# First stage of a hybrid transformer block as one pass over the blocks of k, with packed weight slabs and weights loaded further ahead

## The chip, the cores and the metric

The kernel runs on one core of a Trainium2 chip. The metric is the device time of one execution in microseconds (us), as the median of several runs. The profile is one further execution; "the span" is the time from its first to its last instruction. Engines are PE (matmuls; PEld is its weight load), DVE (VectorE), ACT (ScalarE), POOL (GpSimd) and SP (which issues most DMAs). PSUM has eight banks of 128 x 512 fp32; a matmul writes into one of them.

## The reference, cut to what matters

```python
def block(x, p, w):                          # S = 512 tokens, D = 1024, one layer
    h = rms_norm(x, ln1_g)                   # fp32
    z = h @ w_in                             # mq mk mv mo mi mf | aq akc avc aks avs akw avw ag
    m = mlstm(mq, mk, mv, mi, mf)            # 4 heads of 128, chunks of 64
    a = nsa(aq, akc, avc, aks, avs, akw, avw, ag, ...)   # 8 heads of 64 in 2 groups:
                                             # compressed, selected and window keys
    x = x + concat(m, a) @ w_out
    x = x + convffn(rms_norm(x, ln2_g))      # width 2048, 3 taps
    return rms_norm(x + ple_gate(...), final_g)

def compress(t, pe, w1, w2):                 # for akc and avc: blocks of 32 tokens, stride 16
    return gelu((blocks(t) + pe) @ w1) @ w2
```

Every product is made in fp32 accuracy from three products of a high and a low part: high x high, low x high and high x low.

## The kernel before, in words

The change touches the first 97 us of the kernel, up to the first attention scores (`s_3b`). There the work is a list of jobs (`Stream`), each the product of one packet of weights with all 512 tokens. A job's weights are loaded by SP into one of two buffers (tag `raw`), ACT copies the high part out (`...h`), DVE subtracts to get the low part (`...l`), and PE runs the three products. While a job runs, only the next one is prepared (`AHEAD`), so a load is issued when a `raw` buffer has been read by ACT and DVE.

- `tok0` to `tok3`, two blocks of k each: token-major columns (selected and window values `avs`, `avw`, gates), 288 wide, into four banks (`psA`, tiles `ptm`), one per 128 tokens.
- `c0`, `c1` (the inputs `akc`, `avc` of the compression), `k0`, `k1` (keys), `q00`, `q01` (queries): 128 columns each, feature-major into one bank (`pc`, `pk`, `pq`), 24 matmuls of 512 columns.
- `w00` to `w11` (tiles `cw00` to `cw11`): first matrix of the compression of akc (0) and avc (1), each in two halves.
- `m0` to `m3` (tiles `mv0` to `mv3`): the values of the mLSTM, token-major, into four banks.

`ORDER` lists them: c0 k0 c1 k1 q00 w00 q01 w01 m0 w10 m1 w11 m2 m3. Events run between jobs by estimated time (`st.after`), on engines that each work strictly in their written order. The row factors of the norm come from the squares (`sq`, `acc`), a matmul `n1ps`, a Newton iteration on DVE (`n1v` to `n1yc`), and a matmul `n1pb` that spreads them for feature-major results (`n1rb`, copied by ACT). `token_evac` scales the token-major results (`V` by ACT and DVE, `gz` by DVE). `cmp_evac` scales a result `pc` (`zc`), moves it by four DMAs on ACT's queue into `cA` (lines 409 and 410), adds the positions (`cX`, four pieces on DVE) and splits the sum (`cXh` on ACT, `cXl` on DVE). `mlstm_gates` transposes `gz` on PE (`pgt`), and makes running sums on DVE (two scans); `mlstm_gate_columns` transposes the sums on PE (`pgc`) and DVE copies them (`gcol`). `cmp_gelu` (tile `hc`) and `cmp_turn` (a transpose `pct` on PE, copied to `gt`) follow the last half of a compression. `pgt`, `pgc`, `pct` and `pc2` share one PSUM bank, V, which holds one of them at a time:

```python
def cmp_turn(kv, h2):
    pt = pV(f"pct{kv}")
    TE.transpose(pt[:, 0:62], h2, ident[0:62, 0:62])
```

Evacuated keys and queries are copied to their places by DMAs on POOL (line 386).

Of the kernel before, what the change touches and what calls it, by code (L numbers as in the profile page):

```python
# [27 lines left out]
ORDER = "c0 k0 c1 k1 q00 w00 q01 w01 m0 w10 m1 w11 m2 m3"  # L28
T_TE = 4.0
T_GC = 14.0  # L30
T_CT = 6
# [8 lines left out]
GATES = "k0"  # L40
AHEAD = (1, 1)
# [12 lines left out]
C_G1, C_G2, C_G3, C_GF = 0, 8, 16, 24  # L54
C_CW, C_CB = 32, 80
C_MG = 96
C_PK, C_PV = 100, 116
C_VALID = 132
N_COLS = 133
# [7 lines left out]
def hybrid_block_kernel(ctx: ExitStack, tc: tile.TileContext, a, out):  # L67
# [39 lines left out]
    cols = consts.tile([128, N_COLS], F32, name="cols")  # L107
    xbuf = main.tile([128, KB, S], F32, tag="B16", bufs=3, name="xT")
# [8 lines left out]
    def split(name, src_ap, shape):  # L117
        raw = wpool.tile(shape, F32, tag="raw", bufs=2, name=name + "r")
        hi = wpool.tile(shape, F32R, tag="hi", name=name + "h")
        lo = wpool.tile(shape, F32R, tag="lo", name=name + "l")  # L120
        n = 1 if name == "tok0" else shape[1]
        for i in range(0, shape[1], n):
            nc.sync.dma_start(raw[:, i:i + n], src_ap[:, i:i + n])
            SE.activation(hi[:, i:i + n], raw[:, i:i + n], AF.Copy)
            VE.tensor_sub(lo[:, i:i + n], raw[:, i:i + n], f32(hi[:, i:i + n]))
        return hi, lo

# [5 lines left out]
    class Stream:  # L133
        """The matrix products in their order on the tensor engine; events run between them."""

        def __init__(self):
            self.jobs, self.ready, self.cur, self.done = [], [], None, set()
            self.now, self.events, self.debt = 0.0, [], 0.0
# [3 lines left out]

        def prepare(self, depth):
            while len(self.ready) < depth and self.jobs:
                name, src, shape, run = self.jobs.pop(0)
                self.ready.append((name, run, split(name, src, shape)))
# [10 lines left out]
        def step(self):  # L157
            if self.cur is None:
                self.prepare(1)
                if not self.ready:  # L160
                    return None
                name, run, w = self.ready.pop(0)
                self.cur = (name, run(*w))
                self.prepare(AHEAD[self.now > 100])
            try:
                t = next(self.cur[1])
            except StopIteration:
                self.done.add(self.cur[0])
# [69 lines left out]
    def newton_rsqrt(v, w, name):  # L238
        """1 / sqrt(v): a first guess from the bits, a step of third order, which leaves 8/3 of it, and Newton's."""
# [71 lines left out]

    psA = four("ptm")
    for c in range(4):
        st.add(f"tok{c}", a["w_tok"][:, 2 * c:2 * c + 2], [128, 2, 288], tokens_job(psA, 2 * c, 288))
    nc.sync.dma_start(cols, a["cols"])
    nc.sync.dma_start(xbuf[:, 0], a["xT"][:, 0])
    st.prepare(1)
    nc.sync.dma_start(xbuf[:, 1], a["xT"][:, 1])
    for c in range(4):
# [7 lines left out]
        if c == 0:  # L327
            load_consts()
# [21 lines left out]
    def gemm(ps, wh, wl, kw, rh, rl, kx, first=True, last=True, n=slice(0, S)):  # L350
        """kw, kx: the blocks of the weights and of the activations; the low parts of the weights come last."""
# [23 lines left out]
    mixa = main.tile([128, 2, 4, S], F32R, tag="mixa", name="mixa")  # L375
# [101 lines left out]
    # queries: [high; low] for the first pass, [high; position and mask rows] for the second  # L477
# [89 lines left out]
    # mLSTM gates: the running sum of log f, the running maximum, and their columns by token  # L567
# [210 lines left out]
    nc.sync.dma_start(X, a["xT"])  # L778
# [362 lines left out]
def _layouts(inp):  # L1141
# [10 lines left out]
    def percol(v):  # L1152
# [3 lines left out]
    arr["xT"] = c(x.T.reshape(8, 128, S).transpose(1, 0, 2))  # L1156
# [5 lines left out]
    order = ["aks", "akw", "akc", "avc", "aq", "mq", "mk", "mo"]  # L1162
    arr["w_in"] = c(blocks(np.concatenate([cut[n] for n in order], 1)))
    tok = np.concatenate([cut[n] for n in ("avs", "avw", "mi", "mf", "ag")], 1)
    arr["w_tok"] = c(tok.reshape(8, 128, 288).transpose(1, 0, 2))
# [25 lines left out]
    arr["mask"] = np.where(q <= p, 0, NEG).astype(f)
# [30 lines left out]
```

## Time and profile before

| | |
|---|---|
| time, median of 3 runs | 652.88 us (652.25 to 653.68) |
| span of the profiled execution | 651.60 us |
| PE busy | 96% of the span |
| DVE busy | 65% |
| ACT busy | 48% |
| first 80 us: PE busy | 68.68 of 80 us |

The profiled execution's time is known as its span, 651.60 us; it lies 1.28 us under the median of the runs, which contain what lies around the span. Busy shares are means over all stages. What the change moves lies in the first 97 us, so its worth is read from the waits of that stretch and from what PE does there, at which granted clock.

### The profile page before, as it was taken

The page shows a single profiled execution, that of the slowest core. Times are in us where ns is not written, and L with a number is a line of the kernel's source. Part 1 is how long each engine was busy: PE and PEld are TensorE (multiplying, and loading weights), DVE is VectorE, ACT ScalarE, POOL GpSimd, SP SyncE. Part 2 cuts the span into 40 slices and gives each one's busy share as a digit, 9 for nine tenths or more (in the row PEclk, how much of TensorE's full clock was granted, in tenths as well). Part 3 has the DMA queues.
Part 4 walks back from the last instruction along what each step waited for, and adds up shares of the span by engine and source line. Part 5 has one row for each costly group of instructions (what it writes and reads, how often), then busy time and mean ns, then how long its engine had stood idle before and what let it go on. Part 6 is the DMA issues. An engine that isn't in the chain of part 4 may idle for free.

```text
span 651.6 us, 8628 instructions
## 1 busy us (share of the span) xinstructions
PE 626.2 (96%) x3090; PEld 507.3 (78%) x3090; DVE 423.0 (65%) x862; ACT 311.9 (48%) x650; POOL 51.2 (8%) x112
## 2 busy tenths in 40 slices
PE   6899899999999999999999999999999999999993
PEld 6787777777777776787878888888888888888892
DVE  4697538888877977686586555555555434345866
ACT  5544336667657656465545333333333223234542
POOL 1113104211111100000000000000000000000003
PEclk9999799999999999999999999999999999999997
DMA  7676945511112152212233333333333333333203
GB/s 224 183 185 158 209 127 114 114 34 33 55 44 65 34 188 70 66 33 69 82 109 98 97 98 98 97 98 97 98 97 98 97 98 98 97 97 103 92 2 129
DMA packets 22083, 64.85 MB, mean 100 GB/s; under 512 B 2832, under 2 KB 6032, under 8 KB 21844
## 3 DMA queue, kind: packets, MB, share of 16 engines
q1 hardware_dynamic: 18120, 57.55, 30.1%
q0 software_dynamic: 3136, 5.57, 4.9%
q10 hardware_dynamic: 784, 1.18, 0.7%
q8 instruction: 24, 0.39, 0.3%
q14 instruction: 19, 0.16, 0.1%
HBM read 56.42 MB, written 2.10 MB: 90 GB/s over the span
## 4 chain that ended last, share of the span: by engine, by line
PE 80%; DVE 9%; DMA 5%; ACT 3%; issue 2%; SPq 0%; DVEq 0%; POOL 0%; ACTq 0%
PE pu L354 8%; PE pu L355 8%; PE pu L358 8%; PE pd L354 5%; PE pd L355 4%; PE pd L358 4%; PE pt L709 2%; PE pmq L355 2%; PE pmq L358 2%; PE pmq L354 2%; PE pv L717 2%; PE ms L878 2%; PE pmv L299 1%; PE mo L887 1%; PE pg L346 1%
## 5 line engine op out<-in xcount | busy, mean ns | idle before, releaser
L712 ACT ACTIVATE ph<-pt 128x512 fp32r<-128x512 f32 x40 | 23.7, 597 | 20.9 <-PE pt L709 19.5
L1000 ACT ACTIVATE u<-zv 128x512 fp32r<-128x512 f32 x16 | 10.1, 633 | 45.1 <-DVE zv L998 45.1
L713 DVE TENSOR_TENSOR pl<-pt,ph 128x512 fp32r<-128x512 f32 x40 | 27.1, 683 | 6.3 <-ACT ph L712 6.1
L997 DVE TENSOR_TENSOR zv<-pu,n2rb 128x512 f32<-128x512 f32 x16 | 11.1, 691 | 31.0 <-PE pu L358 31.0
L681 POOL TENSOR_SCALAR E<-E,rr 128x512 f32<-128x512 f32 (+3 forms) x32 | 20.3, 634 | 130.5 <-DVE rr L678 87.8
L709 PE MATMUL pt<-ident,E 128*128 128x128 f32 x160 | 27.7, 276 | 0.4 <-DVE E L683 0.3
L987 DVE TENSOR_TENSOR zg<-pu,n2rb 128x512 f32<-128x512 f32 x16 | 11.1, 692 | 26.0 <-PE pu L358 24.6
L1013 DVE TENSOR_TENSOR X<-pd,X 128x512 f32<-128x512 f32 x8 | 5.5, 692 | 31.9 <-PE pd L358 31.9
L709 PEld LDWEIGHTS pt<-ident,E 128*128 128x128 f32 x160 | 19.8, 141 | 7.2 <-DVE E L683 2.1
L990 ACT ACTIVATE cv<-zg,cols 128x512 f32<-128x512 f32 x16 | 13.1, 816 | 20.1 <-DVE zg L987 20.1
L675 ACT ACTIVATE E<-s,nm 128x384 f32<-128x384 f32 (+2 forms) x48 | 22.1, 470 | 0.0
L993 ACT ACTIVATE cv<-cv 128x512 f32<-128x512 f32 x16 | 10.1, 631 | 24.9 <-DVE cv L992 24.9
L986 POOL MEMSET zg<- 128x2 f32 x16 | 1.5, 99 | 245.2 <-DVE cv L992 151.1
L234 DVE TENSOR_TENSOR acc<-acc,sq 128x512 f32<-128x512 f32 (+1 forms) x30 | 19.1, 637 | 1.6 <-ACT sq L230 1.0
L230 ACT ACTIVATE sq<-X 128x512 f32<-128x512 f32 (+1 forms) x24 | 13.5, 561 | 11.0 <-DVE X L1054 11.0
L717 PE MATMUL pv<-ph,V 128*128 128x512 f32 x40 | 18.7, 467 | 0.0
L346 PE MATMUL pg<-x3h,wres 128*128 128x256 f32 x64 | 18.3, 285 | 0.0
L347 PE MATMUL pg<-x3l,wres 128*128 128x256 f32 x64 | 18.1, 283 | 0.0
L348 PE MATMUL pg<-x3h,wres 128*128 128x256 f32 x64 | 18.1, 283 | 0.0
L1001 DVE TENSOR_TENSOR u<-zv,u 128x512 fp32r<-128x512 f32 x16 | 11.1, 692 | 10.5 <-ACT u L1000 10.5
L1094 POOL TENSOR_TENSOR X<-X,n40rb 128x256 f32<-128x256 f32 (+1 forms) x5 | 4.8, 994 | 155.5 <-ACT n40rb L283 155.5
L719 PE MATMUL pv<-pl,V 128*128 128x512 f32 x40 | 16.7, 418 | 0.0
(1077 smaller groups left out, 2044.7 us busy)
## 6 DMA issues: line engine op xcount, KB each, us to landing
Q<-hlq POOLq DMA_DIRECT2D x24, 128.0 KB, 5.8
X<-in_xT SPq DMA_DIRECT2D x1, 2048.0 KB, 7.6
wgr<-in_w_pg SPq DMA_DIRECT2D x4, 512.0 KB, 4.2
xT<-in_xT SPq DMA_DIRECT2D x3, 512.0 KB, 6.5
K<-hlk POOLq DMA_DIRECT2D x12, 128.0 KB, 4.6
out_y<-X SPq DMA_DIRECT2D x5, 256.0 KB, 2.2
out_y<-X SPq DMA_DIRECT2D x5, 128.0 KB, 1.7
Q<-in_qaug POOLq DMA_DIRECT2D x2, 272.0 KB, 6.7
```

Source lines behind the costliest of these rows:

```text
L234: return VE.tensor_add(acc[:, :n], acc[:, :n], sq[:, :n])
L346: TE.matmul(ps, wh[:, kw], rh[:, kx, n], start=first, stop=False)
L347: TE.matmul(ps, wh[:, kw], rl[:, kx, n], start=False, stop=False)
L354: TE.matmul(ps, wh[:, w], rh[:, x, n], start=first and j == 0, stop=False)
L355: TE.matmul(ps, wh[:, w], rl[:, x, n], start=False, stop=False)
L358: TE.matmul(ps, wl[:, w], rh[:, x, n], start=False, stop=last and j == len(kx) - 1)
L675: SE.activation(e, p, AF.Exp, bias=nm[:, b:b + 1], accum_out=rs[:, b:b + 1])
L681: GE.tensor_scalar(e, e, rr[:, b:b + 1], 0.0, op0=ALU.mult, op1=ALU.add)
L709: TE.transpose(pt[:, r * 128:(r + 1) * 128], Es[r][:, c0:c0 + 128], ident)
L712: SE.activation(ph, pt, AF.Copy)
L713: VE.tensor_sub(pl, pt, f32(ph))
L717: TE.matmul(pv, vs, ph, start=first, stop=False)
```

## The change

The host's arrays are repacked. `xg` is the input with the gain of the first norm as a column behind each block of k. `w_s1` has, for each block of k, a slab of 672 columns: the 288 token-major ones, then `akc`, `aks` and `avc`. The small constants go into one array (`cols`, 515 columns), loaded last. Slab 0 is loaded by two DMAs on ACT's queue, all else by SP.

PE starts with nine idle matmuls of 128 x 512 on zeros in bf16 into bank V. Then one pass over the blocks of k in seven banks: for each of the first four blocks (`KO`) 12 token-major matmuls into the four banks `psA` and 9 feature-major ones into `pc0`, `pk0` and `pc1`. The last four blocks follow bank by bank: `first_rest(0)`, the statistics, `first_rest(1)`, `n1pb`, `first_rest(2)`, then the token-major matmuls. `c0`, `c1` and `k0` (and `tok0` to `tok3`) are no jobs any more.

The other loads are issued three jobs ahead (`LOADS`), into four extra 16-KB buffers (`rawx`, in the place of `mixa`, until `mv3` is loaded) besides the two `raw`. The row factors and the evacuations of `pc0` and `pk0` now come in front of the token-major ones. The gates are made by an event 5 us (`T_GATES`) after `token_evac`, and their columns 14 us (`T_GC`, as before) after that.

```diff
-ORDER = "c0 k0 c1 k1 q00 w00 q01 w01 m0 w10 m1 w11 m2 m3"
-T_TE = 4.0
+ORDER = "k1 w00 q00 w01 q01 w10 m0 w11 m1 m2 m3"
+W1 = 288 + 3 * 128
+KO = 4
+NWARM = 9
 T_GC = 14.0
+T_GATES = 5.0
-GATES = "k0"
-AHEAD = (1, 1)
+LOADS = 3
...
+    nc.sync.dma_start(xbuf[:, 0], a["xg"][:, 0])
+    nc.scalar.dma_start(s1raw[0][:, 0, 0:288], a["w_s1"][:, 0, 0:288])
+    nc.scalar.dma_start(s1raw[0][:, 0, 288:W1], a["w_s1"][:, 0, 288:W1])
+    for k, n in ((1, 1), (2, 2), (4, 2), (6, 2)):
+        nc.sync.dma_start(s1raw[k], a["w_s1"][:, k:k + n])
+        nc.sync.dma_start(xbuf[:, k:k + n], a["xg"][:, k:k + n])
+    nc.sync.dma_start(cols, a["cols"])
+    idle = consts.tile([128, 512], BF, name="idle")
+    VE.memset(idle, 0.0)
+    pidle = pV("idle")
+    for _ in range(NWARM):
+        TE.matmul(pidle, idle[:, 0:128], idle, start=True, stop=True)
...
+    def load(name, src_ap, shape):
+        raw = None
+        if early[0]:
+            turn[0] += 1
+            if turn[0] % 6 < 4:
+                raw = early[0][:, turn[0] % 6].rearrange("p (a b) -> p a b", a=shape[1])
+        if raw is None:
+            raw = wpool.tile(shape, F32, tag="raw", bufs=2, name=name + "r")
+        nc.sync.dma_start(raw, src_ap)
+        return raw
...
-                self.prepare(AHEAD[self.now > 100])
+                self.prepare(1)
+                if early[0]:
+                    self.load(LOADS)
...
-    for c in range(4):
-        if c < 3:
-            nc.sync.dma_start(xbuf[:, 2 * c + 2:2 * c + 4], a["xT"][:, 2 * c + 2:2 * c + 4])
-        for k in (2 * c, 2 * c + 1):
-            last = SE.activation(xh[:, k], xbuf[:, k], AF.Copy, scale=cols[:, C_G1 + k:C_G1 + k + 1])
-            VE.scalar_tensor_tensor(xl[:, k], xbuf[:, k], cols[:, C_G1 + k:C_G1 + k + 1], f32(xh[:, k]),
-                                    op0=ALU.mult, op1=ALU.subtract)
-        st.until(f"tok{c}")
+    pairs = ((xh, hi1), (xl, hi1), (xh, lo1))
     for k in range(KB):
-        sq = square(xbuf[:, k], k, acc1)
-        behind(sq, last, "the splits come first")
+        last = first_split(k)
+        if k > 1:
+            square(xbuf[:, k - 2, 0:S], k - 2, acc1)
+        for x, w in pairs if k < KO else ():
+            for t in range(NT):
+                first_tok(k, t, x, w, k == 0 and w is hi1 and x is xh, False)
+            for j in range(3):
+                first_feat(k, j, x, w, k == 0 and w is hi1 and x is xh, False)
...
+    def first_rest(j):
+        for x, w in pairs:
+            for k in range(KO, KB):
+                first_feat(k, j, x, w, False, k == KB - 1 and w is lo1)
+
+    first_rest(0)
     rc1 = rstd_stats(acc1, "n1")
...
-    st.after(T_TE, token_evac)
-    st.until(GATES)
-    mlstm_gates()
-    st.after(T_GC, mlstm_gate_columns)
-    st.until("q01")
-    psM.extend(four("pmv"))
+    early[0] = main.tile([128, 4, 1024], F32, tag="mixa", name="rawx")
+    st.load(2)
+    first_rest(1)
+    rb1 = rstd_rows(rc1, "n1")
+    cmp_evac(0)(psF[0])
+    key_evac(0)(psF[1])
+    first_rest(2)
+    cmp_evac(1)(psF[2])
+    st.prepare(1)
+    st.load(LOADS)
+    for x, w in pairs:
+        for k in range(KO, KB):
+            for t in range(NT):
+                first_tok(k, t, x, w, False, k == KB - 1 and w is lo1)
+    token_evac()
+    st.after(T_GATES, mlstm_gates)
+    st.after(T_GATES + T_GC, mlstm_gate_columns)
     st.until("mv3")
+    mixa = main.tile([128, 2, 4, S], F32R, tag="mixa", name="mixa")
```

The first place is PE around the gate columns. Before, the eight transposes `pgc` of the gates stand inside the products of `q00`, ahead of the first half of the compression of akc:

```order
L358 MATMUL pq_552<-x1h,q00l 128x512 x2
L598 MATMUL pgc<-ident,gi 128x4 x4
L598 MATMUL pgc<-ident,gt 128x4 x4
L358 MATMUL pq_552<-x1h,q00l 128x512 x6
L432 MATMUL pc_606<-cw00h,cXh_384 62x128
```

In the change the same transposes stand in the first half of the compression of avc (`cw10`), shortly ahead of the transpose `pct` of the compression of akc and of the values `mv0` (`ident` is now a part of `cols`):

```order
L490 MATMUL pc_698<-cw10h,cXh_398 62x128
L491 MATMUL pc_698<-cw10h,cXl_400 62x128
L653 MATMUL pgc<-cols,gi 128x4 x4
L653 MATMUL pgc<-cols,gt 128x4 x4
L495 MATMUL pc_698<-cw10l,cXh_398 62x128 x2
L515 MATMUL pct_725<-cols,hc_643 128x62
L495 MATMUL pc_698<-cw10l,cXh_398 62x128 x6
L332 MATMUL pmv_743<-mv0h,x1h 128x512
```

So `pgc` has moved past `q00`, `w00`, `w01` and `q01`, and `pct`, which takes the same bank, now follows it after two matmuls.

The second place is DVE's copy of these columns, `gcol`. Before, it stands after the keys of the second group and before the queries:

```order
L391 TENSOR_TENSOR zk_535<-pk_510,n1rb 128x512
L125 TENSOR_TENSOR cw00l<-cw00r,cw00h 128x1024
L382 TENSOR_TENSOR hlk_537<-zk_535,hlk_537 128x512
L600 COPY gcol<-pgc 128x32
L485 SCALAR_TENSOR_TENSOR zq_589<-pq_552,n1rb 128x512
L125 TENSOR_TENSOR q01l<-q01r,q01h 128x1024
```

In the change it stands behind the queries of both jobs, the splits of `cw10` and `mv0` and the gelu of the compression:

```order
L440 TENSOR_TENSOR hlq_605<-zq_603,hlq_605 128x512
L479 TENSOR_TENSOR cXl_400<-cX_393,cXh_398 128x992
L153 TENSOR_TENSOR cw10l<-rawx,cw10h 128x1024
L505 TENSOR_TENSOR hc_643<-hc_643 62x128
...
L510 TENSOR_TENSOR hc_643<-hc_643 62x128
L543 SCALAR_TENSOR_TENSOR zq_681<-pq_656,n1rb 128x512
L153 TENSOR_TENSOR mv0l<-rawx,mv0h 128x1024
L440 TENSOR_TENSOR hlq_683<-zq_681,hlq_683 128x512
L655 COPY gcol<-pgc 128x32
L517 COPY gt_727<-pct_725 128x62
```

`gcol` is thus the last of this piece, and the copy of `pct` comes right behind it.

The third place is DVE at the row factors. Before, one split (`k0l`) stands between the last addition of squares and the Newton iteration:

```order
L234 TENSOR_TENSOR acc_91<-acc_91,sq 128x512
L125 TENSOR_TENSOR k0l<-k0r,k0h 128x1024
L267 TENSOR_SCALAR n1v<-n1ps 128x4
```

In the change two splits (`k1l`, `cw00l`) stand there, one of them ahead of the last addition:

```order
L265 TENSOR_TENSOR acc_121<-acc_121,sq 128x512
L153 TENSOR_TENSOR k1l<-rawx,k1h 128x1024
L265 TENSOR_TENSOR acc_121<-acc_121,sq 128x512
L153 TENSOR_TENSOR cw00l<-rawx,cw00h 128x1024
L298 TENSOR_SCALAR n1v<-n1ps 128x4
```

The weights of both are now loaded into `rawx` instead of into the two `raw` buffers.

## Rows read from the trace of the kernel before

**Rows 1.** The page's busy time: us, share of the span, instructions.

```profile
PE 626.2 (96%) x3090; PEld 507.3 (78%) x3090; DVE 423.0 (65%) x862; ACT 311.9 (48%) x650; POOL 51.2 (8%) x112
```

**Rows 2.** Waits of PE, first 140 us: total us, times, longest.

```profile
PE pmv L299 <- ACT mv0h L124: 3.1, 1, 3.1
PE n1pb L280 <- issue: 1.9, 1, 1.9
PE pc L354 <- ACT c0h L124: 0.6, 1, 0.6
```

**Rows 3.** Timeline of PE: start us, us, engine, line, out<-in [idle before <-releaser].

```profile
5.63 0.61 PE L299 MATMUL ptm<-tok0h,x1h 128*128 128x288 f32 x1 [5.63 <-ACT tok0h L124]
...
12.04 0.29 PE L300 MATMUL ptm<-tok1h,x1l 128*128 128x288 f32 x1
12.17 0.29 PE L299 MATMUL ptm<-tok1h,x1h 128*128 128x288 f32 x1
...
67.06 0.79 PE L299 MATMUL pmv<-mv0h,x1h 128*128 128x512 f32 x1 [3.07 <-ACT mv0h L124]
...
73.69 1.98 PE L304 MATMUL pmv<-mv0l,x1h 128*128 128x512 f32 x8
...
77.31 0.44 PE L299 MATMUL pmv<-mv1h,x1h 128*128 128x512 f32 x1
...
96.79 0.39 PE L658 MATMUL s_3b<-K,Q 128*128 128x512 f32 x1
```

**Rows 4.** The chain that ended last, at 58 us: start, us, what.

```profile
58.39 7.45 DMA mv0r<-in_w_mv
65.95 1.06 ACT mv0h L124
```

**Rows 5.** Windows: busy us of PE, PEld, DVE, ACT, POOL; granted clock, DMA share, GB/s.

```profile
30.00:40.00 10.00, 9.59 (x49) 7.71 (x49) 7.60 (x18) 4.03 (x8) 0.59 (x2) 1.00 0.52 148
45.00:50.00 5.00, 5.00 (x24) 4.13 (x23) 4.90 (x6) 3.00 (x4) 0.00 (x0) 1.00 0.92 245
50.00:60.00 10.00, 9.95 (x66) 8.12 (x65) 8.90 (x15) 4.58 (x6) 3.92 (x8) 1.00 0.35 88
60.00:70.00 10.00, 6.93 (x43) 5.72 (x42) 4.76 (x5) 2.64 (x3) 4.05 (x9) 0.82 1.29 251
70.00:80.00 10.00, 10.00 (x55) 8.15 (x55) 4.58 (x9) 3.65 (x5) 1.19 (x3) 0.84 0.98 218
```

**Rows 6.** Timeline of SP, its second DMA issue: start us, us.

```profile
1.19 0.42 SPq L316 DMA_DIRECT2D xT<-in_xT  x1
```

**Rows 7.** Lines 409 and 410, the copies into cA, and their landing.

```profile
L409 ACTq DMA_DIRECT2D cA<-zc x4: 469/568/620, 36.0 to 45.7; - x4
DMA to landing us min/median/max: 2.3/2.5/4.2
L410 ACTq DMA_DIRECT2D cA<-zc x4: 610/616/1987, 36.5 to 46.4; - x4
DMA to landing us min/median/max: 2.4/4.5/5.4
```

**Rows 8.** DVE by line and form, first 100 us: busy us, mean ns, idle before.

```profile
L416 DVE TENSOR_TENSOR cX<-cA,cols 128x248 f32<-128x248 f32 x8 | 4.2, 568 | 0.0
L559 DVE SCALAR_TENSOR_TENSOR V<-ptm,n1yc,V 128x256 fp32r<-128x256 f32 x4 | 1.9, 478 | 0.0
L125 DVE TENSOR_TENSOR q01l<-q01r,q01h 128x1024 fp32r<-128x1024 f32 x1 | 1.2, 1203 | 0.0
L584 DVE TENSOR_TENSOR_SCAN gt<-gf,zeroc 4x512 f32<-4x512 f32 x1 | 1.2, 1212 | 0.0
L485 DVE SCALAR_TENSOR_TENSOR zq<-pq,n1rb 128x512 f32<-128x512 f32 x2 | 1.4, 676 | 0.0
L561 DVE TENSOR_SCALAR gz<-ptm,n1yc 128x32 f32<-128x32 f32 x4 | 1.0, 242 | 0.0
L452 DVE TENSOR_TENSOR hc<-hc 62x128 f32<-62x128 f32 x2 | 0.6, 285 | 0.1
```

More of the change, by code (lines that the diff above doesn't have):

```diff
@@ L52 @@
 GELU_A = 0.044715
[L54 to L59, printed above, removed]
+C_G2, C_G3, C_GF = 0, 8, 16
+C_CW, C_CB = 24, 72
+C_MG = 88
+C_PK, C_PV = 92, 108
+C_VALID = 124
+C_SEL, C_GB = 125, 129
+C_ID, C_NEG, C_MASK = 131, 259, 387
+N_COLS = 515
 def f32(ap):
@@ L115, in hybrid_block_kernel, with split @@
     GE.memset(epsc, EPS)
-    def split(name, src_ap, shape):
-        raw = wpool.tile(shape, F32, tag="raw", bufs=2, name=name + "r")
+    turn = [0]
+    def load(name, src_ap, shape):
[8 more added lines that the diff above has]
+        return raw
+    def split(name, raw, shape):
         hi = wpool.tile(shape, F32R, tag="hi", name=name + "h")
         lo = wpool.tile(shape, F32R, tag="lo", name=name + "l")
[L121 to L125, printed above, removed]
+        SE.activation(hi, raw, AF.Copy)
+        VE.tensor_sub(lo, raw, f32(hi))
         return hi, lo
+    early = [None]
     def behind(later, sooner, why, wait=False):
@@ L136, in __init__ @@
         def __init__(self):
-            self.jobs, self.ready, self.cur, self.done = [], [], None, set()
+            self.jobs, self.loaded, self.ready, self.cur, self.done = [], [], [], None, set()
             self.now, self.events, self.debt = 0.0, [], 0.0
@@ L141, in add, with load @@
             self.jobs.append((name, src, shape, run))
+        def load(self, depth):
+            while len(self.loaded) < depth and self.jobs:
+                name, src, shape, run = self.jobs.pop(0)
+                self.loaded.append((name, load(name, src, shape), shape, run))
+                if name == "mv3":
+                    early[0] = None
         def prepare(self, depth):
-            while len(self.ready) < depth and self.jobs:
-                name, src, shape, run = self.jobs.pop(0)
-                self.ready.append((name, run, split(name, src, shape)))
+            while len(self.ready) < depth and (self.jobs or self.loaded):
+                self.load(1)
+                name, raw, shape, run = self.loaded.pop(0)
+                self.ready.append((name, run, split(name, raw, shape)))
         def after(self, us, fn):
@@ L295, in run @@
         def run(wh, wl):
+            if k0 == 0:
+                ps.extend(four("pmv"))
             for k, i in ((k, i) for k in (k0, k0 + 1) for i in range(NT)):
@@ L329, in hybrid_block_kernel, with first_split @@
-    for k in range(KB):
-        sq = square(xbuf[:, k], k, acc1)
-        behind(sq, last, "the splits come first")
+    psF = [pG("pc0"), pG("pk0"), pSb("pc1")]
+    hi1 = main.tile([128, 6, W1], F32R, tag="B16", bufs=3, name="hi1")
+    lo1 = main.tile([128, 6, W1], F32R, tag="B16", bufs=3, name="lo1")
+    def first_split(k):
+        g = xbuf[:, k, S:S + 1]
+        SE.activation(xh[:, k], xbuf[:, k, 0:S], AF.Copy, scale=g)
+        raw = s1raw[min(k, k // 2 * 2) if k > 1 else k]
+        raw = raw[:, k % 2 if k > 1 else 0]
+        for c0, c1 in (((0, 288), (288, W1)) if k == 0 else ((0, W1),)):
+            i = SE.activation(hi1[:, k % 6, c0:c1], raw[:, c0:c1], AF.Copy)
+        VE.scalar_tensor_tensor(xl[:, k], xbuf[:, k, 0:S], g, f32(xh[:, k]), op0=ALU.mult, op1=ALU.subtract)
+        for c0, c1 in (((0, 288), (288, W1)) if k == 0 else ((0, W1),)):
+            VE.tensor_sub(lo1[:, k % 6, c0:c1], raw[:, c0:c1], f32(hi1[:, k % 6, c0:c1]))
+        return i
@@ new lines, in first_tok, with first_feat @@
+    def first_tok(k, t, x, w, start, stop):
+        TE.matmul(psA[t][:, 0:288], x[:, k, t * 128:(t + 1) * 128], w[:, k % 6, 0:288], start=start, stop=stop)
+        st.spend(0.135)
+    def first_feat(k, j, x, w, start, stop):
+        TE.matmul(psF[j], w[:, k % 6, 288 + 128 * j:416 + 128 * j], x[:, k], start=start, stop=stop)
+        st.spend(0.23)
+    pairs = ((xh, hi1), (xl, hi1), (xh, lo1))
+    for k in range(KB):
+        last = first_split(k)
[6 more added lines that the diff above has]
+                first_feat(k, j, x, w, k == 0 and w is hi1 and x is xh, False)
@@ L332, in hybrid_block_kernel @@
+    for k in (KB - 2, KB - 1):
+        square(xbuf[:, k, 0:S], k, acc1)
+    wload.close()
+    def first_rest(j):
[3 more added lines that the diff above has]
+    first_rest(0)
     rc1 = rstd_stats(acc1, "n1")
@@ L1161, in _layouts @@
     cut = dict(zip(names, np.split(w, np.cumsum(sizes)[:-1], axis=1)))
-    order = ["aks", "akw", "akc", "avc", "aq", "mq", "mk", "mo"]
+    order = ["akw", "aq", "mq", "mk", "mo"]
     arr["w_in"] = c(blocks(np.concatenate([cut[n] for n in order], 1)))
-    tok = np.concatenate([cut[n] for n in ("avs", "avw", "mi", "mf", "ag")], 1)
-    arr["w_tok"] = c(tok.reshape(8, 128, 288).transpose(1, 0, 2))
+    first = np.concatenate([cut[n] for n in ("avs", "avw", "mi", "mf", "ag", "akc", "aks", "avc")], 1)
+    arr["w_s1"] = c(first.reshape(8, 128, W1).transpose(1, 0, 2))
     arr["w_mv"] = c(cut["mv"].reshape(8, 128, 512).transpose(1, 0, 2))
```

70 lines of the change are left out of this document (27 added, 43 removed).

## The prediction

> **What bounds the kernel now.** I read the page's busy times first, then the waits of PE, then the windows of the first 97 us, then PE's own timeline. PE is busy for 96% of the span [rows 1], so a gain can only come from three things: PE's few waits, stretches in which its clock is granted at half, and its start. The reader is to see three waits of PE behind the start: 0.6 us for `c0h`, 1.9 us in front of `n1pb`, and 3.07 us for `mv0h` [rows 2, 3]. The last one is a load: `mv0r` is issued at 58.39 and lands 7.45 us later, and `mv0h` is copied from 65.95 [rows 4]. It was issued late because its buffer came free only when DVE had split `q01`.
>
> Two stretches run at the lower level of the clock (1.2 of 2.4 GHz). From PE's first matmul at 5.63 to 12.04, 25 token matmuls start in 6.41 us; from 12.04 on they start 0.13 apart [rows 3]. So 24 to 25 of them cost about 3.2 us too much. After the wait for `mv0h`, 16 matmuls start from 67.06 to 73.69, in 6.63 us; the eight after them take 1.98 with the last one's 0.39, some 0.227 each [rows 3], so 16 would need 3.6, and 3.0 are lost. The granted clock is 0.82 from 60 to 70 and 0.84 from 70 to 80 [rows 5]; (0.18 + 0.16) x 10 / 0.5 = 6.8 us at the lower level; as this ended shortly before 73.69, it began near 66.7, some 2.6 us into the wait that began at 67.06 - 3.07 = 64.0. The wait of 1.9 us, which `n1pb` ends, shows no fall behind it: 1.00 from 30 to 40 [rows 5].
>
> DVE is the second bound: 4.90 us of 5 from 45 to 50, 8.90 of 10 from 50 to 60 [rows 5].
>
> **The change part by part.** I follow the time F at which `s_3b` starts, now 96.79 [rows 3]; behind it the order is the same, so I take the difference over to the end.
>
> *Same work.* The one pass has the matmuls that `tok0` to `tok3`, `c0`, `c1` and `k0` had: 96 token and 72 feature ones, 96 x 0.13 + 72 x 0.227 = 28.8 us, no more and no fewer. Per block of k that is 3.6 us of PE. What it needs in that time: on DVE the low parts of x and of the slab and an addition, 0.7 + 0.8 + 0.7 by the rows of 512 and 1024 columns [rows 8]; of DMA 0.26 MB of x and 0.34 of the slab, 169 GB/s where 245 were seen [rows 5]. So I charge nothing for splits and loads behind the first block; if they came at half that pace, PE would wait about 0.8 us per block, some 3 us over the four.
>
> *Start.* x goes out first on SP, ahead of `cols`, not second at 1.19 [rows 6]. One issue takes 0.42 there, and I take that off the start: 5.63 to 5.2. With no gain there it is 5.6.
>
> *Idle matmuls.* They need no load. The slow matmuls behind 67.06 took (6.63 - 0.23) / 15 = 0.427 each, so nine fill some 3.9 us, from about 1.1 (about when SP and ACT are at their second instruction, an estimate) to 5.0. In both places where the clock rose, matmuls had run for some 6.4 us before. If the idle ones count, it rises near 7.5, and 2.3 us of work run at half: 1.15 lost rather than 3.2. Bounds: they count for nothing (3.2 lost), or the clock is up at the first real matmul (0).
>
> *Waits removed.* The statistics are made behind the third bank's rest with the additions done early, and `mv0r` has a buffer in `rawx` and goes out near 25, 30 us ahead. I drop 0.6, 1.9, 3.07 and the 3.0 of the clock behind it. The longest load seen is 7.45 [rows 4], so three jobs of 3 to 5 us each cover it.
>
> *Clean sum.* 96.79 - 5.63 = 91.16; less 0.6, 1.9, 3.07, 3.0 and 3.2 leaves 79.4 of PE. With the new start F = 5.2 + 1.15 + 79.4 = 85.75, 11 us earlier. That holds only if nothing new waits.
>
> *What is late next: DVE.* PE now reaches everything earlier, but DVE has the same work, and in a new order. `n1pb` ends near 27.5: 5.2 + 1.15, then 48 x 0.13 + 36 x 0.227 = 14.4 for the first four blocks, 24 x 0.227 = 5.4 for two banks' rests, and about 1.3 for the two small products and what lies between. Then `n1rb` 0.6, `zc` 0.68, the copies into `cA` (issues of about 0.6 each on ACT, landing 2.3 to 2.5 [rows 7]), four `cX` pieces at 0.57 [rows 8], and `cXh`, about 1. Only behind that does ACT issue the second compression's copies, near 36.6; their first pair lands near 39.4. Behind their `cX` stand, on DVE, `V`, `gz`, the gates and all else down to `gcol`: 42 instructions. By the rows: 4 `cX` at 0.57, 4 `V` at 0.48, 4 `gz` at 0.24, six splits of about 1024 columns and two scans at 1.2, thirteen of the size of `zq` at 0.68, five of the gelu near 0.26, and four short ones of 1.0 together: 2.3 + 1.9 + 1.0 + 9.7 + 8.8 + 1.3 + 1.0 = 26.0 [rows 8]. Successive ones overlap by 0.07, some 2.9 in all; against that DVE waits for PE's `pgt`, for ACT's tables and tanh. At the busy share that it had from 45 to 60, (4.90 + 8.90) / 15 = 0.92 [rows 5], 23.1 become 25.1. I take 26.1, because two of its waits are new (PE reaches `pgt` only in `w00`), so `gcol` ends at 65.5. Bounds: no waits, 62.5; 2 us more, 67.5.
>
> *The new wait of PE.* `pct` takes the bank of `pgc`, so it waits for `gcol`. Before, `gcol` was done long before it. On PE, from `pct` to `s_3b` remain 0.5 of `cw10`, 24 matmuls of `mv0` at 0.227 (5.4), and 96.79 - 77.31 = 19.5 [rows 3]: 25.4. By the clean sum PE reaches `pct` at 85.75 - 25.4 = 60.35, and with about 1.7 of smaller waits ahead of it (for `gz` at `pgt`, for the second `pgt`, for `q01l`) at 62.05. It waits until 65.5, 3.4 us. F = 65.5 + 25.4 = 90.9: 5.9 us gained, not 11.
>
> *The clock behind it.* The wait of 3.07 brought a fall, that of 1.9 none [rows 2, 3, 5]. 3.4 is beyond the first. As in the wait for `mv0h`, 2.6 us in, the clock would fall and stay down for 6.8 us, of which 0.8 are still idle and 6.0 run at half: about 2.9 lost. F = 93.8, 3.0 earlier. The bounds are 0 and 3.2.
>
> *A rule that speaks against it.* Of cycling through banks, the rows show this: the token matmuls of before take four banks in turn, and from 12.04 on start 0.13 apart at clock 1.00 [rows 3, 5]; so the seven-bank pass costs 28.8 us here by the rows. The Trainium skill, page "TensorE: Matmul & The Clock Gate", section "A second HAM failure mode: psum-queue depth-cycling", says that a kernel cycling through PSUM banks in each iteration let PE pause between its groups often enough that the clock swung between its levels. The four-bank rows here show no such swing; no run shows seven banks.
>
> **The sum.** 96.79 - 93.8 = 3.0 gained. The profiled execution's span would go from 651.6 to 648.6; it lies 1.28 under the median of the runs, and I take the same distance: 652.88 - 3.0 = 649.9.
>
> **The rivals.**
> *No fall of the clock* (the wait at `pct` is there, but shorter than about 2.6 us, or the clock holds): F = 90.9, 647.0. For it: DVE without waits would make `gcol` at 62.5 and leave a wait of 0.5, then F = 87.9 and 644. Against: DVE was never without waits.
> *The second copies late by 2 us*: landing 4.5 is the median of line 410 [rows 7]. `gcol` at 67.5, F = 95.8, 651.9: no difference that can be measured. About 0.2%, 1.3 us, is what a measurement of this kernel can tell from no change.
> *The idle matmuls count for nothing*, the part of the change that would not do what it says: 2.05 more at the start. PE then comes later to `pct` and some of it is hidden there, but at most I put it at the full 2.05: 651.9.
> *Slower.* Two copies into `cA` stand in series on DVE's path. Line 410 landed after 5.4 at the longest, while loads ran [rows 7], and now three loads run beside them. Both at 5.4 rather than 2.4 put the chain 6 us later, DVE's start from 39.4 to 45.4, and the time at 655.9. It decides from 4.3 us later (start past 43.7): then the time is over 654.2. Against: line 409's median is 2.5.
> *The seven banks swing the clock*: half of the pass's 28.8 at the lower level adds 14.4 to 649.9: 664.3. I give it 0.02, since the four-bank rows show nothing of it. It is what the rule of the Trainium skill cited above ("TensorE: Matmul & The Clock Gate") would do.
>
> **How the numbers follow.** Forecast 649.9: 0.52. No fall, 647.0: 0.24. Copies late, 651.9: 0.10. Idle matmuls for nothing, 651.9: 0.06. Slower, 655.9: 0.06. Bank swing: 0.02. Faster by over 0.2% (under 651.58): the first two, 0.76. Within: 0.16. Slower: 0.08. The forecast's own range is 648.5 to 651 (its bounds of `gcol` by 1 us either way). The range must hold 0.8: from 646, somewhat under the second case, for a `gcol` 1 us earlier without a fall, up to 652.4, beyond the third and fourth; that leaves out the slower cases and the no-wait end.
>
> **What would show it.** In the profile after: PE's first real matmul near 5.2 and 0.13 spacing from about 7.5; no wait at `n1pb` nor for `mv0h`; a wait of some 3.4 us at `pct`, released by DVE's `gcol` near 65.5; granted clock near 0.8 in the 10 us behind it; `s_3b` near 93.8. The forecast is wrong if the wait at `pct` is under 2.6 or missing (then 647 or less), if DVE's `cX` of the second compression starts well after 39.4, if PE waits inside the pass for slabs or splits, or if the stage behind `s_3b` takes another time than before.

## The result

The changed kernel takes 657.73 us (median of 9 runs, 656.69 to 659.17) where the kernel before takes 652.88 beside it (650.76 to 656.88): ratio 1.0074, 95% interval 1.0052 to 1.0096. On a second chip the ratio was 1.0039 (1.0012 to 1.0067). It is slower by 0.4 to 0.7%. The profiled execution has a span of 657.4 us, 5.8 more than that of before. It took 659.17 us, the longest of the nine, so the account below is of about 1 us more than the 4.85 between the medians.

Where do the 5.8 us lie? In the tile `s_3b`, with which the stage of the change ends (form: count, ns min/median/max, first and last start):

```profile
L724 PE MATMUL s_3b<-K,Q x8: 392/394/501, 102.2 to 232.6; 128*128 128x512 f32 x8
```

It starts at 102.2, not at 96.79 [rows 3]: 5.4 of the 5.8 us are lost ahead of it. The waits of PE in the changed kernel, first 140 us (us, times, longest):

```profile
PE pgt L632 <- DVE gz L616: 8.1, 2, 6.6
PE pct L515 <- DVE gcol L655: 3.0, 1, 3.0
PE idle L127 <- DVE ones L247: 1.2, 1, 1.2
PE pc L368 <- ACT hi L357: 0.9, 1, 0.9
...
PE pq L417 <- DVE q01l L153: 0.5, 1, 0.5
PE pgt L632 <- DVE gi L633: 0.4, 1, 0.4
```

The three waits of before [rows 2] are gone, and so is the slow start. But in their place stand 8.1 us at `pgt` for `gz` and 3.0 at `pct` for `gcol`. The windows of the changed kernel (columns as in [rows 5]) show the clock behind both:

```profile
10.00:20.00 10.00, 10.00 (x59) 8.92 (x58) 9.89 (x15) 10.00 (x18) 3.09 (x3) 1.00 0.87 351
...
40.00:50.00 10.00, 3.38 (x16) 2.34 (x15) 3.98 (x8) 3.65 (x6) 2.47 (x9) 0.77 0.58 133
50.00:60.00 10.00, 8.12 (x49) 6.64 (x49) 8.09 (x17) 5.57 (x8) 2.06 (x5) 0.72 0.25 69
60.00:70.00 10.00, 9.47 (x69) 7.76 (x69) 9.73 (x13) 4.50 (x6) 4.08 (x8) 1.00 0.82 174
70.00:80.00 10.00, 6.97 (x35) 5.59 (x33) 5.09 (x12) 2.83 (x4) 3.05 (x6) 0.66 0.76 154
```

From 40 to 60 the clock is down for (0.23 + 0.28) x 10 / 0.5 = 10.2 us, from 70 to 80 for 6.8. PE's timeline has the start and both waits:

```profile
1.19 3.72 PE L127 MATMUL idle<-idle 128*128 128x512 bf16 x9 [1.19 <-DVE ones L247]
5.24 0.79 PE L364 MATMUL ptm<-hi,x1h 128*128 128x288 f32 x4 [0.33 <-ACT hi L357]
...
49.43 0.37 PE L632 MATMUL pgt<-cols,gz 128*4 128x128 f32 x1 [6.62 <-DVE gz L616]
...
51.79 0.80 PE L632 MATMUL pgt<-cols,gz 128*4 128x128 f32 x3 [1.47 <-DVE gz L616]
...
74.18 0.36 PE L515 MATMUL pct<-cols,hc 62*128 62x62 f32 x1 [3.03 <-DVE gcol L655]
```

Why `gz` is late stands in the timeline of DVE:

```profile
31.05 0.69 DVE L464 TENSOR_TENSOR zc<-pc,n1rb 128x512 f32<-128x512 f32 x1 [0.86 <-PE pc L368]
37.79 1.08 DVE L474 TENSOR_TENSOR cX<-cA,cols 128x248 f32<-128x248 f32 x2 [6.05 <-DMA cA<-zc]
...
47.69 1.04 DVE L474 TENSOR_TENSOR cX<-cA,cols 128x248 f32<-128x248 f32 x2 [4.92 <-DMA cA<-zc]
48.65 0.47 DVE L614 SCALAR_TENSOR_TENSOR V<-ptm,n1yc,V 128x256 fp32r<-128x256 f32 x1
49.04 0.24 DVE L616 TENSOR_SCALAR gz<-ptm,n1yc 128x32 f32<-128x32 f32 x1
...
73.95 0.18 DVE L655 COPY gcol<-pgc 128x32 f32<-128x32 f32 x1
```

DVE waits 6.05 us for the first compression's copies into `cA` and 4.92 for the second's, and `V` and `gz` stand behind the second. The copies' own lines (ns of one issue, starts, landing), which answer to [rows 7]:

```profile
L467 ACTq DMA_DIRECT2D cA<-zc x4: 469/570/757, 29.6 to 41.8; - x4
DMA to landing us min/median/max: 3.2/6.6/7.7
L468 ACTq DMA_DIRECT2D cA<-zc x4: 603/616/618, 30.2 to 42.6; - x4
DMA to landing us min/median/max: 5.3/6.7/7.5
```

The median landing is 6.6 and 6.7 us; it was 2.5 and 4.5. Each line holds copies of both compressions. Taken apart by their time of issue, the first compression's four landed after 6.9 to 7.7 us and the second's after 3.2 to 6.4; in the kernel before it was after 2.3 to 2.4 and after 2.6 to 5.4.

### The profile page after: what moved, and what is told of

Its sections match the earlier page's. It is cut to its first block, busy times and chain, and to the rows that moved or that the text cites. A ratio compares the mean times of both kernels' runs of the same rounds, so it can differ in the third digit from the quotient of the medians.

```text
span 657.4 us, 8625 instructions
## 1 busy us (share of the span) xinstructions
PE 628.7 (96%) x3099; PEld 507.0 (77%) x3099; DVE 423.1 (64%) x864; ACT 311.4 (47%) x651; POOL 53.7 (8%) x112
## 4 chain that ended last, share of the span: by engine, by line
PE 82%; DVE 9%; DMA 4%; ACT 3%; issue 2%; ACTq 0%; DVEq 0%
PE pu L413 8%; PE pu L417 8%; PE pu L414 8%; PE pd L413 4%; PE pd L414 4%; PE pd L417 4%; DMA cA<-zc 2%; PE pt L775 2%; PE pmq L414 2%; PE pmq L417 2%; PE pmq L413 2%; PE pv L783 2%; PE ms L944 2%; PE pg L405 1%; PE pmv L332 1%
## 5 line engine op out<-in xcount | busy, mean ns | idle before, releaser
L1063 DVE TENSOR_TENSOR zv<-pu,n2rb 128x512 f32<-128x512 f32 x16 | 11.1, 691 | 31.3 <-PE pu L417 31.3
L775 PE MATMUL pt<-cols,E 128*128 128x128 f32 x160 | 28.0, 276 | 0.4 <-DVE E L749 0.3
L1079 DVE TENSOR_TENSOR X<-pd,X 128x512 f32<-128x512 f32 x8 | 5.5, 691 | 31.7 <-PE pd L417 31.7
L775 PEld LDWEIGHTS pt<-cols,E 128*128 128x128 f32 x160 | 19.8, 140 | 7.5 <-DVE E L749 2.4
L1056 ACT ACTIVATE cv<-zg,cols 128x512 f32<-128x512 f32 x16 | 13.1, 816 | 19.8 <-DVE zg L1053 19.8
```

Of the source, the lines that this page charges most:

```text
L775: TE.transpose(pt[:, r * 128:(r + 1) * 128], Es[r][:, c0:c0 + 128], ident)
```

## The experiments

Theory A: the five weight loads that the change sends early (`cw01`, `q01`, `cw10`, `mv0`, `cw11`, 512 KB each, issued between 20 and 25 us) share the DMA engines with the copies and make them land late; DVE's order then carries that to `gz`, and PE's clock falls behind the wait. Rival B: DVE is saturated by the same work, whatever its order. Rival C: POOL's moves of keys (six of 128 KB) and rows of queries (272 KB) delay the copies. The first four runs shared one chip, the next four another, the last four a third. In the table, `s_3b` is its start, "adds" are the starts of the first and second compression's first `cX`, and the waits are PE's, all from each one's profile; the ratio is to the kernel before.

| run | median us | ratio, interval | s_3b | adds | at pgt | at pct |
|---|---|---|---|---|---|---|
| the change, first run | 657.73 | 1.0074 (1.0052 to 1.0096) | 102.2 | 37.79, 47.69 | 8.5 | 3.0 |
| e1 second sums later | 655.43 | 1.0006 (0.998 to 1.0031) | 99.0 | 38.20, 50.19 | 3.6 | 2.4 |
| e2 five loads held | 652.42 | 0.9956 (0.9933 to 0.9979) | 95.0 | 32.61, 40.15 | 2.8 | 2.7 |
| e3 T_GC 25 | 654.63 | 1.0005 (0.9979 to 1.003) | 98.3 | 38.66, 47.73 | 8.6 | 1.5 |
| e4 no idle matmuls | 659.01 | 1.0037 (1.0014 to 1.0061) | 100.5 | 38.04, 47.03 | 5.9 | 3.0 |
| e5 = e2 + e3 | 648.88 | 0.9889 (0.9841 to 0.9937) | 91.3 | 32.66, 40.00 | 3.2 | 1.5 |
| e6 held, e1, e3 | 650.54 | 0.9927 (0.9898 to 0.9956) | 94.0 | 32.58, 46.21 | 1.2 | 0.9 |
| e8 = e6, no idle matmuls | 652.28 | 0.9957 (0.9928 to 0.9985) | 94.4 | 34.33, 47.98 | 1.2 | 0.9 |
| e7 the change again | 658.03 | 1.0039 (1.0012 to 1.0067) | 101.3 | 37.64, 46.72 | 6.0 | 3.0 |
| e9 three loads held | 652.44 | 0.9952 (0.9925 to 0.9979) | 97.5 | 34.23, 41.99 | 3.1 | 3.0 |
| e12 only moves held | 654.64 | 0.9994 (0.9963 to 1.0025) | 97.0 | 37.43, 43.28 | 4.1 | 2.7 |
| e10 = e5 + moves held | 647.13 | 0.9879 (0.9837 to 0.9921) | 89.7 | 32.62, 38.45 | 1.1 | 1.5 |
| e11 = e5 again | 649.32 | 0.9921 (0.9891 to 0.9951) | 91.7 | 32.58, 40.21 | 3.2 | 0.4 |

**e1.** The second compression's additions go behind the gates' reads of `pgt` on DVE.

```diff
-            VE.tensor_scalar(dst, pt[0:4], gbias[:, bcol:bcol + 1], None, op0=ALU.add)
+            gate = VE.tensor_scalar(dst, pt[0:4], gbias[:, bcol:bcol + 1], None, op0=ALU.add)
...
+        later[0](gate)
```

`later[0]` holds the additions of `cmp_evac(1)`, `cXh` and `cXl`, which are ordered behind `gate`.

> One change to the changed kernel: the four position additions of the second compression (cX of avc) stand on DVE behind the two gate additions that read pgt, not ahead of V and gz. Theory A (DVE's written order makes V and gz wait for copies into cA that land late): V and gz start near 43.5 rather than 48.65, PE's waits at pgt shrink from 8.5 us to 2 to 4, and the time falls by 4 to 6 us, to 652 to 654; the wait at pct stays near 3. Rival B (DVE is simply saturated by the same work, whatever its order): the wait at pgt shrinks, but as much comes back at pct and at the splits, and the time stays within 1.5 us of 657.7.

The wait at `pgt` fell from 8.5 us (6.0 in e7, the change again) to 3.6 and `s_3b` from 102.2 (101.3) to 99.0. That is under theory A's saving by 1 us or more, and more than B's 1.5: DVE's order was a part. Of what is left at `pgt`, 2.3 us are a wait for ACT's `V`. ACT makes it from 43.63 on, right behind its issues of the second copies, and these stand behind the late first ones (first add still at 38.20). A wait of 1.7 us for `q01l` is new.

**e2.** The five loads wait for the second compression's additions.

```diff
+HOLD = {n: 1 for n in ("cw01", "q01", "cw10", "mv0", "cw11")}
...
-        nc.sync.dma_start(raw, src_ap)
+        dma = nc.sync.dma_start(raw, src_ap)
+        if name in HOLD:
+            behind(dma, copied[HOLD[name]], "loads behind the copies", True)
```

`copied[1]` is the last of the second compression's additions.

> One change to the changed kernel: the weight loads from cw01 on (five of 512 KB, issued from 20 to 25 us) wait until the second compression's copies have been added up on DVE. Theory A (the weight loads share the DMA engines with the copies into cA and make them land after 5 to 7.7 us): landings near 2.5 to 3.5, cX of avc starts near 40 rather than 47.7, PE's wait at pgt falls from 8.5 us to under 2, time 650 to 653. Rival C (the copies are late by themselves, or for the moves of keys on POOL): landings stay at 5 or more, and the time stays at 657 or rises, since the held loads come later.

As theory A had it. The timeline of DVE in e2:

```profile
32.61 1.09 DVE L478 TENSOR_TENSOR cX<-cA,cols 128x248 f32<-128x248 f32 x2 [0.86 <-DMA cA<-zc]
...
40.15 1.07 DVE L478 TENSOR_TENSOR cX<-cA,cols 128x248 f32<-128x248 f32 x2 [2.57 <-DMA cA<-zc]
```

DVE waits 0.86 us for the first copies, not 6.05: all four landed after 2.3 to 2.4 us. POOL's first moves go out at 33.07 in both kernels, so they are not what delayed these. The second compression's copies still took 3.3 to 5.7 us. `s_3b` starts 7.2 us sooner than in the first profile of the change and 6.3 sooner than in e7's, with the same work on DVE, so B does not explain it; and PE waits for none of the loads, which go out 24 us later.

**e3.** `T_GC` is 25 instead of 14.

```diff
-T_GC = 14.0
+T_GC = 25.0
```

> One change to the changed kernel: T_GC 25 instead of 14, so that the gate columns (pgc, gcol) come behind the transpose pct of the first compression. Theory A (PE waits at pct for gcol because they share a bank, and the clock falls behind that wait): the wait of 3.0 us and the stretch at half clock from 72.8 to 79.5 go, 4.5 to 5.5 us less, near 652.7. Rival B (DVE is late anyway): PE waits at pct for hc or at mv0 for mv0l for about as long, and the clock falls all the same: within 1.5 us of 657.7.

```profile
PE pgt L632 <- DVE gz L616: 8.2, 2, 6.7
PE pct L515 <- DVE hc L510: 1.5, 1, 1.5
```

With `pgt` untouched, the wait at `pct` halves and is now for `hc`, which `pct` reads. The clock stays at 1.00 from 70 to 80 there, and `s_3b` starts 3.9 us sooner than in the change (3.0 sooner than in e7): what the bank cost, with the clock behind it. The median fell by 3.1 us, short of the 4.5 to 5.5 expected, as 1.5 us of waiting stay at `pct`.

**e4.** No idle matmuls.

```diff
-NWARM = 9
+NWARM = 0
```

> One change to the changed kernel: no idle matmuls. If they bring the clock up before the data comes, PE's first matmuls start at half clock without them for about 6.4 us, as before the change: 2 to 3.2 us more at the start, and since PE waits later for DVE, which does not hang on PE's start, part of that is hidden at pgt: 0.5 to 3 us more in all, 658 to 660.5. If they do nothing, the first matmuls are as fast without them and the time stays at 657.7.

The change had 1.0074 and 1.0039 on two other chips, and this run's 1.0037 has an interval of 0.005 about it: in the changed kernel the idle matmuls are worth nothing that can be told, since PE, sooner or later at `pgt`, waits there for `gz`.

**e5 and e11.** e2 and e3 together, on two chips.

> The two single changes together: the weight loads behind the copies into cA, and T_GC 25. If the two waits of PE (at pgt behind late copies, at pct behind gcol) are separate costs, the second is saved on top of the first: s_3b starts 2 to 4 us sooner than at 95.0, the wait at pct falls from 2.7 to about 1 (for hc), the ratio to the kernel before is 0.989 to 0.993. If DVE's saturation is the limit and the waits only change places, the ratio stays at that of the first change alone, 0.9956.

> The version with the five loads held and T_GC 25 once more, on the chip of the runs beside it: ratio to the kernel before between 0.986 and 0.993, s_3b near 91.3.

The savings add up: 91.3 and 91.7, against 95.0 with the loads held alone. This version beats both kernels.

**e6 and e8.** e5 with the hold only up to the first compression's additions (`HOLD` with 0), and e1; e8 without idle matmuls.

> Three changes together: loads held until the first compression's copies have landed, the second compression's additions behind the gates' reads of pgt, T_GC 25. If V and gz no longer wait for any copy, PE's waits at pgt fall under 1 us in all, the clock does not fall from 40 to 60, and s_3b starts at 88 to 91: ratio 0.985 to 0.990. If the loads of the five weights, now in the company of the second copies, are late or DVE is the limit, it is no better than with the loads held and T_GC 25 alone.

> As the run before with the three changes, but without the idle matmuls. With PE's start on the path again, the half clock of the first 6.4 us of work should cost 1.5 to 2.8 us (0.2% to 0.4%) against the run with them. If the stretch behind it waits for DVE or for copies, the cost is hidden: under 0.7 us.

A miss: the wait at `pgt` fell to 1.2 us, but the loads now ran beside the second copies, of which one landed after 13.5 us. DVE waited for it 3.03 us, and PE 2.0 us for `q01h`. The other three of the second copies landed after 7.8 to 13.1 us. `s_3b` came at 94.0, 2.7 later than in e5; between the medians it is 1.7. Letting the loads go sooner moved the wait. Against e8, on the same chip, the idle matmuls are worth 1.7 us (0.27%) here by the medians. The two profiles show only 0.4 at `s_3b`, as the clock fell in e6's (0.78 and 0.88 from 50 to 70) and not in e8's (1.00). e8's first matmuls of 512 columns start 0.43 apart:

```profile
6.76 0.63 PE L372 MATMUL pc<-x1h,hi 128*128 128x512 f32 x1
7.19 0.63 PE L372 MATMUL pk<-x1h,hi 128*128 128x512 f32 x1
```

**e7.** The change unaltered.

> The changed kernel unaltered, on the same chip as the runs beside it, as their yardstick: ratio to the kernel before between 1.005 and 1.0095 as measured first. PE waits again at pgt for gz, 6 to 9 us, behind copies into cA that land after 5 us or more.

The ratio, 1.0039, is under the 1.005 expected, and the wait at `pgt`, 6.0 us, is at the low end. The start differs from the first profile: the nine idle matmuls ran here too, but the first real ones are at the lower level, four token matmuls in 1.33 us and not in 0.79, and the upper level comes only near 10.4.

```profile
5.65 1.33 PE L364 MATMUL ptm<-hi,x1h 128*128 128x288 f32 x4 [0.44 <-ACT hi L357]
```

So the first copy goes out at 31.16 and not at 29.62. The first add comes at 37.64 all the same: the loads beside the copies set it, not PE's start.

**e9.** Only `cw10`, `mv0` and `cw11` are held.

```diff
+HOLD = {n: 1 for n in ("cw10", "mv0", "cw11")}
```

> The changed kernel with three of the five weight loads held behind the second compression's copies (cw10, mv0, cw11), while cw01 and q01 go early beside them as in the change. Theory A (late landing by the company of weight loads): landings between 2.8 to 3.2 (five held) and 5.5 to 6.6 (none held), s_3b between 95 and 101, ratio between 0.9956 and 1.004. If a single load were enough to make the copies late, or only the last ones mattered, it lies at one of the ends.

The first add comes at 34.23, 1.6 us behind e2, but so does the issue of the first copy. It is at 29.63 in e2; this is e9:

```profile
31.17 0.53 ACTq L471 DMA_DIRECT2D cA<-zc  x1
...
34.23 1.09 DVE L478 TENSOR_TENSOR cX<-cA,cols 128x248 f32<-128x248 f32 x2 [0.94 <-DMA cA<-zc]
```

This profile, of the longest of the ten executions, has the slow start of e7's. The first four copies landed after 2.3 to 2.4 us, as in e2, and the medians are the same (652.44 and 652.42): the two loads that still go early cost the copies nothing. They landed 7.9 and 9.3 us after their issue, the second near 31.1, just as the copies went out. In the change the last of the five, issued at 24.88, landed after 12.6 us, near 37.5, and the first copies land about then (37.3 to 38.4). So it is one of the ends that the expectation named: what counts is the loads still under way when the copies go.

**e12.** POOL's moves of the first keys and its second load of query rows wait for the second compression's additions; the weight loads are as in the change. The evacuation of the keys is written behind the second compression's, which the lines below do not show (in e10 too).

```diff
-        nc.gpsimd.dma_start(dst, src)
+        dma = nc.gpsimd.dma_start(dst, src)
+        if 1 in copied and len(moved) < 6:
+            behind(dma, copied[1], "moves behind the copies", True)
...
+                if g == 1:
+                    behind(aug, copied[1], "moves behind the copies", True)
```

> The changed kernel with the weight loads early as in the change, but POOL's six moves of the first keys and its second load of query rows held behind the second compression's additions (the keys' evacuation is written behind that compression's). If the weight loads make the copies late (theory A), the first landing stays at 5 to 7 us, V and gz start after 45, PE waits 4 us or more at pgt: ratio 1.000 to 1.007. If POOL's moves do (rival C), landings fall to about 3 and the ratio to about 0.996.

```profile
37.43 1.08 DVE L483 TENSOR_TENSOR cX<-cA,cols 128x248 f32<-128x248 f32 x2 [5.00 <-DMA cA<-zc]
...
43.28 1.06 DVE L483 TENSOR_TENSOR cX<-cA,cols 128x248 f32<-128x248 f32 x2 [0.89 <-DMA cA<-zc]
```

Here theory A and rival C are both right, one for each copy. The first copies stay late without the moves (first add at 37.43, landing after 6.5 to 7.2 us). But the second add follows 5.85 us after the first, where the change needs 9.9 (9.1 in e7): the moves delay the second copies by 3 to 4 us. It is not the order of the evacuations: ACT issues the second copies from 40.3 to 42.1 here and from 40.7 to 42.6 in the change, behind the loads in both, and they land after 2.2 to 2.4 us rather than 3.2 to 6.4.

**e10.** e5 with POOL's moves held too.

> The version with the five loads held and T_GC 25, and POOL's moves of the first keys and the second load of query rows held as well. The second pair of the second copies landed near 43 there, beside these moves. If the moves delay it, it lands near 40, PE's wait at pgt falls from 2.1 us to under 1, s_3b from 91.3 to 89.5 to 90.5, 0.1% to 0.3% less. If not, the time stays within 0.1%.

The timeline of DVE, and the copies of both compressions together (KB of one, median us to landing):

```profile
32.62 1.09 DVE L483 TENSOR_TENSOR cX<-cA,cols 128x248 f32<-128x248 f32 x2 [0.28 <-DMA cA<-zc]
...
38.45 1.09 DVE L483 TENSOR_TENSOR cX<-cA,cols 128x248 f32<-128x248 f32 x2 [0.86 <-DMA cA<-zc]
```

```profile
cA<-zc ACTq DMA_DIRECT2D x4, 128.0 KB, 2.3
...
cA<-zc ACTq DMA_DIRECT2D x4, 127.8 KB, 2.4
```

With neither beside them the copies land after 2.3 and 2.4 us, and the time is the best of all: 647.13, 2.2 us under e11 on the same chip.

## Why the prediction was wrong

**The step that failed** is in "What is late next: DVE": "the copies into `cA` (... landing 2.3 to 2.5)" and, from it, "their first pair lands near 39.4". The sum took the landing of copies that run alone, though the change itself sends 2.5 MB of weights ahead of them and POOL's moves beside the second. Seven of the eight landed after 5.3 to 7.7 us (the other after 3.2), the second compression's first add came at 47.69, 8.3 us late, and all that stood behind it on DVE came late with it. e2, e12 and e10 show each part: with the loads held the first add is 5.0 to 5.2 us sooner, with the moves held the second comes 3 to 4 us sooner after the first. Without either it is at 38.45, near the 39.4 of the sum.

The rest of the sum held. With 47.69 in place of 39.4 and nothing else changed, it has `gcol` done at 47.69 + 26.1 = 73.8 and `s_3b` at 73.8 + 25.4 + 2.9 = 102.1; the profile has 74.13 and 102.2. From their own starts of this add it gives 101.1 for e7 (measured 101.3), 97.7 for e12 (97.0), 96.4 for e9 (97.5) and 94.6 for e2 (95.0).

**The rival that came true** is the slower one, "two copies into `cA` stand in series on DVE's path", at 6 us later and deciding from a start past 43.7. Its place, its cause and nearly its price were right (8.3 us, and 5.4 us slower at `s_3b` where it gave 3.0); its chance of 0.06 was too small. What spoke for it was in the rows: the median landing of line 410 was 4.5 and its longest 5.4 [rows 7]. What spoke against it, line 409's 2.5, is no price of its own: both lines mix the two compressions. In the trace of before, the first four copies landed after 2.3 to 2.4 us on either line, and the second four, issued from 44.57 on behind POOL's moves of 42.23 and beside a load, after 2.6 to 5.4.

The Trainium skill, page "DMA: Bandwidth & Descriptors", section "Issuing engines are not separate DMA queues", says that DMAs started by different engines run on the same 16 engines and interleave. The runs agree: copies issued by ACT land after 2.2 to 2.4 us with neither beside them, after 6.5 to 7.2 beside SP's loads alone (e12) and after 3.3 to 5.7 beside POOL's moves alone (e2).

**Point by point.**
- *Start*: 5.24, as predicted (5.2), but in part by luck: the other profiles of the changed start have 5.43 to 5.84, about the 5.63 of before. A gain of 0.4 is not shown.
- *Idle matmuls*: in this profile they did more than predicted. The first real ones already run at the upper level (four token matmuls in 0.79 us), 4.05 us after the first idle one, so the 1.15 us put down as lost are not; waits of 0.9 and 0.3 for slab 0 took their place. That is not so in each execution: in the profiles of e7 and e9, two of eleven with idle matmuls, the upper level came only near 10.4, and the first copy went out at 31.2, hardly sooner than without idle matmuls (31.7 in e4, 31.3 in e8) and 1.5 to 1.7 later than in the others. In the changed kernel all of it is hidden behind `gz` (e4, e7); in e6 against e8 it is worth 1.7.
- *Seven banks*: no swing. The clock is 1.00 from 10 to 40, and from 7.23 the feature matmuls start 0.23 apart. The rule of the Trainium skill on cycling through PSUM banks ("TensorE: Matmul & The Clock Gate", section "A second HAM failure mode: psum-queue depth-cycling") does not show itself in this pass; the measurement decides.
- *Waits removed*: all three, with the clock's fall behind the last.
- *DVE's chain*: 26.4 us from 47.69 to the end of `gcol` at 74.13, against 26.1 predicted from durations.
- *Waits ahead of `pct`*: 1.7 predicted, 9.0 measured (8.1, 0.4 and 0.5), and a fall of the clock there that was not in the sum. It was down for 10.2 us, of which some 4.3 had work (49.43 to about 55.6, less the waits of 1.47 and 0.41): 2.1 lost.
- *`pct`*: 3.0 for `gcol` against 3.4. The clock fell behind it as foretold: down for 6.8 us, with 5.3 of work from 74.18 on, 2.7 lost against 2.9. But it fell 1.6 us into the wait, not 2.6, and e1's wait of 2.4 at `pct` had a fall behind it too (0.66 from 70 to 80), so the 2.6 that the prediction read from one wait is no bound. e3 removed both.

Followed along PE instead, with the measured terms: 5.24 + 79.4 (clean work) + 1.2 + 9.0 + 2.1 + 3.0 + 2.7 = 102.6, and `s_3b` starts at 102.2. From there on both kernels need the same, 555.2 and 554.8 us. So the gain of 11 us that the clean sum had was real, and it was given back as two waits and two falls of the clock.

## What to carry to other kernels

When a change loads further ahead, look for the short DMAs in which the path runs (here copies within SBUF, 128 KB), and price them with the landing that they have in the company that the change gives them, not with that of a quiet stretch. Loads that have landed by then cost nothing (e9). One that would still be under way, and is early by more than it needs, can be held until the copies are through: here PE waited for none of the five loads held by 24 us, and the stage was 6 to 7 us shorter. An engine that works in its written order passes a late copy on to all that stands behind it, so what PE needs next belongs ahead of what waits for a DMA.

## What was not expected of the hardware

Waits of the same length need not have the same effect on the clock. e5 and e11 are one kernel, and both profiles show waits of 2.1 and 1.1 us at `pgt`. The windows from 40 to 60 of e5, and then of e11:

```profile
40.00:50.00 10.00, 6.85 (x52) 5.58 (x51) 8.43 (x20) 4.40 (x7) 0.00 (x0) 1.00 0.59 205
50.00:60.00 10.00, 9.30 (x59) 7.56 (x57) 8.81 (x11) 7.15 (x10) 3.89 (x8) 1.00 1.04 272
```

```profile
40.00:50.00 10.00, 6.77 (x46) 5.49 (x45) 8.02 (x19) 3.83 (x6) 0.00 (x0) 0.82 0.61 199
50.00:60.00 10.00, 10.00 (x56) 8.32 (x55) 8.83 (x12) 7.27 (x9) 3.49 (x7) 0.84 1.00 277
```

In one the clock stays at 1.00, in the other it is down for 6.8 us behind the same waits. In e8 PE waited longer still, 1.8 us for `q01h` and then 3.1 for `q01l`, and the clock is 1.00 in each window of 10 us from 10 to 100:

```profile
63.98 2.12 PE L421 MATMUL pq<-x1h,q01l 128*128 128x512 f32 x8 [3.13 <-DVE q01l L157]
```

The wait of 3.07 for `mv0h` in the kernel before had a fall behind it [rows 3, 5]. The kernel before spreads over 650.60 to 659.93 us in 21 executions on the last chip, with mean granted clocks from 0.992 down to 0.982, the changed one over 656.54 to 658.75 in 10 on the chip before. Most of the spread goes with the clock. Time at half clock does half the work, so 0.010 of the mean clock over 655 us stands for 6.6 us (an estimate); a straight line through the 25 executions of the kernel before on e7's chip falls by 6.7 us for each 0.010, with a correlation of -0.92. Behind which waits the clock falls in its longer executions is not shown, as no profile of one was taken.
